# A pair of weight casts moved behind a normalisation on ScalarE, between output projection and up projection

## The chip, the cores and the metric

One Trainium2 chip, one core of it. The time is the device time of one execution in microseconds (us); of several executions the median is given. Engines are called by the names of the profile: PE (TensorE), DVE (VectorE), ACT (ScalarE), POOL (GpSimd) and SP (SyncE, which issues the DMAs here).

## The reference

One decoder layer on 512 tokens of width 1024, in float32, then a last norm. What matters here is the passage from the mixing block to the feed-forward block:

```python
merged = gates[:, :, 0] * y_a + gates[:, :, 1] * y_b + gates[:, :, 2] * y_c
x = x + merged @ w_o                                   # 512x1024 @ 1024x1024
x = x + conv_ffn(rmsnorm(x, ln2_g), w_up, conv_w, conv_b, w_down)
return rmsnorm(x, final_g)

def conv_ffn(u, w_up, conv_w, conv_b, w_down):
    h = causal_dwconv(u @ w_up, conv_w, conv_b)        # 512x1024 @ 1024x5632
    a, v = h[..., :2816], h[..., 2816:]
    return (silu(a) * v) @ w_down
```

`rmsnorm(x, g)` is `x * rsqrt(mean(x*x) + 1e-6) * g` along the 1024 columns. The norm with `ln2_g` is the "second norm": nothing of `u @ w_up` can be computed for a token before its whole row of x is there.

## The kernel before

**Products.** Every large product is computed as three: weights and activations are each split into a high part (a cast to the type that TensorE multiplies) and a low part (what the cast left out), and `mm3` adds high times high, high times low and low times high in PSUM. A product of a weight tile thus needs four things in turn: the raw tile by DMA (`fetch`), its high part `wh` (`cast`, on ACT, as two halves), its low part `wl` (`low`, on DVE, raw minus high), and the activations in both parts.

**Jobs and weight tiles.** `program()` lists some hundred jobs. Each has one weight tile of at most 1 MB and a body that issues the products with it. They share ring buffers: 2 raw tiles (`wraw`), 3 high parts (`whp`), 2 low parts (`wlp`). The loop at the end goes through the jobs; for job n, `prepare` makes the low part of tile n+1, the high part of tile n+2, and fetches tile n+3. A fetch has to wait for a raw buffer, which comes free when the low part of tile n+1 has been made. In most jobs the two casts are not issued at once but one at a time, at the next `step()` of the body (`spread`).

**The order of the work.** PE, ACT, DVE and POOL run their instructions in the order in which the program text issues them (`manual_schedule`), so a waiting instruction holds up everything behind it on its engine. SP's DMAs are put in order by the framework, outside that list.

**Around the change.** The output projection (`wo_jobs`) works on token tiles of 128 rows, in pairs: tiles 0 and 1, then 2 and 3, and for each pair on two halves of 512 columns. Each half is two jobs, one for each half of the inner dimension. When a tile's second half is done, `evac` adds it to x (L939) and begins the norm: squares on ACT (`junk`, L306), the product with g on DVE (`xg`, L339), the mean (`v`, L340), the square root on ACT (L341), then on DVE the reciprocal (L343), two small steps, and the scaled rows (`u`, L347). `norm_turn` then transposes the rows on PE (`uT`, L319), casts them to `uh` on ACT (L322) and subtracts to `ul` on DVE (L323). For tiles 2 and 3 the parts of the norm are kept in the list `late` and are issued by the first two jobs of the up projection.

Three jobs are marked `late`: the last of the output projection (`turn_over`), and the first two of the up projection (`opening`, half 0 and half 1). They call `prepare` themselves. With `later=True` it gives back a function, `rest`, that issues the remaining part when it is called. In the last job of the output projection the call stands ahead of all products, and `rest` is called in `evac` of token tile 3, behind the square root of its norm. In the first job of the up projection the call has `now=False` and everything is in `rest`, which is called behind the transposes of token tile 2.

The first two jobs of the up projection compute only the first 256 tokens (L1036): high weight times `uh`, high weight times `ul`, then the transposes of token tile 2 (in the first job) or 3 (in the second), then low weight times `uh`. The other 256 tokens follow for both jobs together (`held`), through `chunk_a` (L221). `step()` and `up_evac` follow each of these.

Of the kernel before, what the change touches and what calls it, by code (L numbers as in the profile page):

```python
# [81 lines left out]
def trunk(ctx: ExitStack, tc, out, x, rel_bias, ln1_g, w_in, b_gate, w_a, pool_w, pool_scale, w_b,  # L82
# [26 lines left out]
    def MM(name):  # L109
        return psum.tile([P, S], F32, name=name, tag="mm")  # L110
# [26 lines left out]
    def flush():  # L137
        todo = second[:]
        second.clear()
        for f in todo:  # L140
            f()

    def step():
        flush()
        for it in list(running):
            try:
                next(it)
            except StopIteration:
                running.remove(it)
        if waiting:  # L150
            it = iter(waiting.pop(0))
            running.append(it)
            try:
                next(it)
            except StopIteration:
                running.remove(it)
# [11 lines left out]
    def fetch(job, cuts=1):  # L168
        raw = job.raw = wraw.tile([P, job.k, job.c], F32, name="raw", tag="raw")
        at = 0  # L170
        for src in job.parts:
            n = src.shape[-1] // cuts
            for i in range(cuts):
                sp.dma_start(raw[:, :, at:at + n], src[:, :, i * n:(i + 1) * n])
                at += n

    def cast(job, cuts=1, spread=False):

        w = job.c // cuts
        job.high = whp.tile([P, job.k, job.c], F32R, name="wh", tag="wh")  # L180

        def high(i):
            o = slice(i * w, (i + 1) * w)
            act.copy(job.high[:, :, o], job.raw[:, :, o])  # L184

        def at(i):
            high(i)
            if i + 1 < cuts:
                second.append(lambda: at(i + 1))

        if spread:
            second.append(lambda: at(0))
            return
        for i in range(cuts):
            high(i)
# [12 lines left out]
    def low(job, cuts=1, eng=None):  # L208
        for _ in lows(job, cuts, eng):
            pass  # L210

    def wsrc(w, k0, k1, c0, c1):
        return w[k0 * P:k1 * P, c0:c1].rearrange("(k p) c -> p k c", p=P)
# [10 lines left out]
    def chunk_a(ps, ws, j, xh, xl, ks, lo=0, hi=S, k0=0):  # L224
        wh, wl = ws
        mm3(ps[:, lo:hi], lambda k: wh[:, k0 + k, j * P:(j + 1) * P],
            lambda k: wl[:, k0 + k, j * P:(j + 1) * P],
            lambda k: xh(k)[:, lo:hi], lambda k: xl(k)[:, lo:hi], ks)
# [769 lines left out]
    def up_evac(m, ps):  # L998
        t = HC[m] = T("hc")
        act.activation(t, ps, AF.Identity, bias=ff["c1"][:, ff["b"] + m:ff["b"] + m + 1], scale=fw(2, m))  # L1000
        for k in range(2):
            sh = 2 - k
            dve.scalar_tensor_tensor(t[:, sh:], ps[:, :S - sh], fw(k, m), t[:, sh:], OP.mult, OP.add)  # L1003
        if m < KF:
            act.activation(t, t, AF.Silu)
            return
        a = HC[m - KF]
        pool.tensor_tensor(a, a, t, OP.mult)  # L1008

        def later():  # L1010
            yield
            k = m - KF
            if k == 0:
                wide.extend(ypool.tile([P, 4, S], F32R, name=n, tag="xs") for n in ("fh", "fl"))
            h, l = (t[:, k, :] for t in wide) if k < 4 else (T("fh", F32R), T("fl", F32R))
            act.copy(h, a)
            dve.tensor_sub(l, a, h.bitcast(F32))
            ACTS[k] = (h, l)

        running.append(later())  # L1020

    def up_jobs():
        held = []

        def opening(job, half):
            def body(ws):
                uh2, ul2 = nxt["uh"], nxt["ul"]
                low = job.prepare(later=True, now=False) if half == 0 else None
                if half == 0:
                    next(late[1])  # L1030
                pss = [MM("pu") for _ in range(2)]

                def product(a, b, i):
                    for j in range(2):
                        for k in range(KD):
                            pe.matmul(pss[j][:, :256], a[:, k, j * P:(j + 1) * P], b[:, k, :256],  # L1036
                                      start=i + k == 0, stop=i == 2 and k == KD - 1)

                product(ws[0], uh2, 0)
                product(ws[0], ul2, 1)  # L1040
                next(late.pop(0), None)
                if low:
                    low()
                product(ws[1], uh2, 2)
                for j in range(2):
                    held.append((ws, j, pss[j], KF * half + j))
                if half == 0:
                    return
                for n, (ws_, j, ps, m) in enumerate(held):
                    chunk_a(ps, ws_, j, lambda k: uh2[:, k, :], lambda k: ul2[:, k, :], range(KD), 256, S)  # L1050
                    if n == 1:
                        job.prepare()
                    up_evac(m, ps)
                    step()
            return body

        for p in range(KF // 2):
            for half in range(2):
                def body(ws, p=p, half=half):
                    uh2, ul2 = nxt["uh"], nxt["ul"]  # L1060
                    for j in range(2):
                        ps = MM("pu")
                        chunk_a(ps, ws, j, lambda k: uh2[:, k, :], lambda k: ul2[:, k, :], range(KD))
                        up_evac(KF * half + 2 * p + j, ps)
                        step()
                c = half * DFF + p * 256
                job = Job([wsrc(w_up, 0, KD, c, c + 256)], KD, 256, body)
                if p == 0:
                    job.late = True
                    job.body = opening(job, half)  # L1070
                yield job
# [65 lines left out]
    weights = [j for j in jobs if isinstance(j, Job)]  # L1137
# [135 lines left out]
    n = 0  # L1273
    for job in jobs:
        if not isinstance(job, Job):
            job.fn()
            continue
        while second:
            flush()
        if n >= 2:  # L1280
            def prepare(n=n, later=False, now=True):

                def high():
                    if n + 2 < len(weights):
                        cast(weights[n + 2], 2, spread=not later)

                def rest():
                    if n + 1 < len(weights):
                        low(weights[n + 1])
                    if not now or not later:  # L1290
                        high()
                    if n + 3 < len(weights):
                        fetch(weights[n + 3])
                if later:
                    if now:
                        high()
                    return rest
                rest()

            if job.late:  # L1300
                job.prepare = prepare
            else:
                prepare()
            job.body(job.split)
        n += 1
# [38 lines left out]
```

## Time and profile before

| what | value |
|---|---|
| median of 3 runs | 1062.61 us (1062.47 to 1064.94) |
| the profiled execution | 1064.09 us, of which the span of the profile is 1062.2 us |
| PE busy | 1045.9 us, 98% |
| DVE busy | 576.8 us, 54% |
| ACT busy | 431.1 us, 41% |
| POOL busy | 135.1 us, 13% |
| mean granted clock of PE | 0.995 of full speed |
| read from HBM | 110.87 MB, 106 GB/s over the span |

Times in the profile are microseconds from the start of the span; mean durations of single instructions are in nanoseconds. A row of the timeline merges neighbouring instructions of one kind and gives their start, the time that they cover and their number. Matmuls are pipelined, and their ends are modelled: a row's length is a little more than the distance to the next row. The part of the span that the change touches lies between 674 and 710 us.

### The profile page before, as it was taken

The page shows a single profiled execution, that of the slowest core. Times are in us where ns is not written, and L with a number is a line of the kernel's source. Part 1 is how long each engine was busy: PE and PEld are TensorE (multiplying, and loading weights), DVE is VectorE, ACT ScalarE, POOL GpSimd, SP SyncE. Part 2 cuts the span into 40 slices and gives each one's busy share as a digit, 9 for nine tenths or more (in the row PEclk, how much of TensorE's full clock was granted, in tenths as well). Part 3 has the DMA queues.
Part 4 walks back from the last instruction along what each step waited for, and adds up shares of the span by engine and source line. Part 5 has one row for each costly group of instructions (what it writes and reads, how often), then busy time and mean ns, then how long its engine had stood idle before and what let it go on. Part 6 is the DMA issues. An engine that isn't in the chain of part 4 may idle for free.

```text
span 1062.2 us, 13018 instructions
## 1 busy us (share of the span) xinstructions
PE 1045.9 (98%) x5268; PEld 874.4 (82%) x5268; DVE 576.8 (54%) x777; ACT 431.1 (41%) x698; POOL 135.1 (13%) x118
## 2 busy tenths in 40 slices
PE   8999999999999999999999999989999999999997
PEld 8878889888788887787888888888888888888885
DVE  5552523245667547667658766556656565532315
ACT  6343412232445633558536224534444444431311
POOL 1580000000000001100161500002111111110100
PEclk9999999999999999999999999989999999999999
DMA  7236233251221365442243337333232323232312
GB/s 237 79 115 179 82 100 107 72 140 50 83 80 60 83 166 158 110 129 81 80 111 119 119 97 263 119 118 101 95 104 81 118 80 119 80 119 69 110 60 79
DMA packets 116426, 115.50 MB, mean 109 GB/s; under 512 B 5235, under 2 KB 101302, under 8 KB 116367
## 3 DMA queue, kind: packets, MB, share of 16 engines
q1 hardware_dynamic: 116367, 114.68, 35.5%
q8 instruction: 41, 0.67, 0.3%
q14 instruction: 18, 0.15, 0.0%
HBM read 110.87 MB, written 2.22 MB: 106 GB/s over the span
## 4 chain that ended last, share of the span: by engine, by line
PE 91%; ACT 2%; issue 2%; DVE 2%; DMA 1%; POOL 0%; SPq 0%; DVEq 0%; ACTq 0%; POOLq 0%
PE pa L221 35%; PE pu L221 22%; PE pb L221 17%; PE pqk L221 9%; PE ps L512 1%; PE ppw L221 1%; PE po L551 1%; PE pt L539 1%; PE pu L1036 1%; ACT wh L184 1%; PE py L808 1%; DVE wl L204 1%; PE pyo L814 1%; DMA raw<-in_w_in_dram 1%; DMA raw<-in_ffn_w_up_dram 0%
## 5 line engine op out<-in xcount | busy, mean ns | idle before, releaser
L204 DVE TENSOR_TENSOR wl<-raw,wh 128x2048 fp32r<-128x2048 f32 (+3 forms) x94 | 219.2, 2333 | 137.9 <-PE pb L221 67.7
L184 ACT CAST wh<-raw 128x1024 fp32r<-128x1024 f32 (+2 forms) x186 | 187.2, 1025 | 109.6 <-PE pb L221 40.8
L221 PE MATMUL pa<-uh,wh 128*128 128x512 f32 x384 | 99.3, 400 | 0.3 <-ACT wh L184 0.3
L1003 DVE SCALAR_TENSOR_TENSOR hc<-pu,fcol,hc 128x510 f32<-128x510 f32 x88 | 65.9, 749 | 55.9 <-ACT hc L1000 54.3
L221 PE MATMUL pa<-ul,wh 128*128 128x512 f32 x384 | 95.0, 389 | 0.0
L221 PE MATMUL pa<-uh,wl 128*128 128x512 f32 x384 | 94.9, 389 | 0.0
L221 PEld LDWEIGHTS pa<-ul,wh 128*128 128x128 f32 x384 | 72.1, 188 | 15.3
L221 PEld LDWEIGHTS pa<-uh,wl 128*128 128x128 f32 x384 | 72.1, 188 | 15.0
L221 PE MATMUL pu<-ul,wh 128*128 128x512 f32 (+1 forms) x352 | 83.5, 379 | 0.0
L221 PE MATMUL pu<-uh,wl 128*128 128x512 f32 (+1 forms) x352 | 83.5, 379 | 0.0
L221 PE MATMUL pu<-uh,wh 128*128 128x512 f32 (+1 forms) x352 | 83.5, 379 | 0.0
L221 PEld LDWEIGHTS pa<-uh,wh 128*128 128x128 f32 x384 | 69.9, 188 | 16.5 <-issue 1.7
L221 PEld LDWEIGHTS pu<-uh,wl 128*128 128x128 f32 x352 | 64.2, 188 | 12.5
L221 PEld LDWEIGHTS pu<-ul,wh 128*128 128x128 f32 x352 | 64.2, 188 | 12.5
L221 PEld LDWEIGHTS pu<-uh,wh 128*128 128x128 f32 x352 | 64.1, 188 | 12.4
L1000 ACT ACTIVATE hc<-pu,fcol,fcol 128x512 f32<-128x512 f32 x40 | 31.2, 780 | 83.5 <-PE pu L221 83.5
L1008 POOL TENSOR_TENSOR hc<-hc 128x512 f32<-128x512 f32 x22 | 31.6, 1435 | 230.1 <-DVE hc L1003 188.1
L787 POOL TENSOR_TENSOR xd<-xc,dec 128x512 f32<-128x512 f32 x6 | 6.4, 1065 | 361.6 <-DVE xc L778 343.0
L533 ACT ACTIVATE sb<-sb,nm 128x128 f32<-128x128 f32 (+1 forms) x72 | 30.1, 419 | 46.9 <-DVE nm L530 33.2
L221 PE MATMUL pb<-wh,fh 128*128 128x512 f32 x176 | 47.7, 389 | 0.0
L221 PE MATMUL pb<-wl,fh 128*128 128x512 f32 x176 | 47.7, 389 | 0.0
L221 PE MATMUL pb<-wh,fl 128*128 128x512 f32 x176 | 47.7, 389 | 0.0
(273 smaller groups left out, 1601.8 us busy)
## 6 DMA issues: line engine op xcount, KB each, us to landing
raw<-in_w_in_dram SPq DMA_DIRECT2D x25, 1024.0 KB
raw<-in_ffn_w_up_dram SPq DMA_DIRECT2D x22, 1024.0 KB
raw<-in_w_in_dram SPq DMA_DIRECT2D x20, 512.0 KB
raw<-in_ffn_w_down_dram SPq DMA_DIRECT2D x10, 1024.0 KB
raw<-in_w_o_dram SPq DMA_DIRECT2D x8, 1024.0 KB
raw<-in_w_in_dram SPq DMA_DIRECT2D x6, 768.0 KB
raw<-in_w_b_dram SPq DMA_DIRECT2D x4, 1024.0 KB
al<-ad SPq DMA_DIRECT2D x16, 256.0 KB
```

The lines of the kernel that those rows point to most:

```text
L184: act.copy(job.high[:, :, o], job.raw[:, :, o])
L204: (eng or dve).tensor_tensor(l[:, :, o], job.raw[:, :, o], h[:, :, o].bitcast(F32), OP.subtract)
L221: pe.matmul(ps, l, r, start=first and n == 0, stop=last and n == total - 1)
L512: pe.matmul(pss[i][:, o:o + w * P], q[r, n * P:(n + 1) * P], k[r, kb * P:(kb + w) * P], start=True, stop=True)
L533: act.activation(sb[:, off:off + w * P], sb[:, off:off + w * P], AF.Exp, bias=nm[:, n, h:h + 1], accum_out=ls[:, n, h:h + 1])
L539: pe.transpose(pt[:, o:o + P], sb[:, o:o + P], eye)
L551: pe.matmul(po[DH * hh:DH * hh + DH, n * P:(n + 1) * P], V[g, kb + i][:, (2 * c + hh) * DH:(2 * c + hh + 1) * DH], probs[2 * c + hh, nb][: ...
L808: pe.matmul(py[DH * i:DH * i + DH, j * P:(j + 1) * P], xc[:, o:o + DH], als[j // 2][:, lo:lo + P], start=True, stop=True)
L814: pe.matmul(po[:, j * P:(j + 1) * P], prev[gi][:, j * P:(j + 1) * P], XS[10 + gi][:, cs], start=True, stop=True)
L1000: act.activation(t, ps, AF.Identity, bias=ff["c1"][:, ff["b"] + m:ff["b"] + m + 1], scale=fw(2, m))
L1003: dve.scalar_tensor_tensor(t[:, sh:], ps[:, :S - sh], fw(k, m), t[:, sh:], OP.mult, OP.add)
L1008: pool.tensor_tensor(a, a, t, OP.mult)
```

## The change

`prepare` loses its parameter `now` and the function `high`. With `later=True` it issues nothing by itself any more; `rest` issues all: the low part of tile n+1, the two casts of tile n+2, the fetch of tile n+3. The first job of the up projection did that already (by `now=False`), and ordinary jobs issue the three in this order too. So what is different is the last job of the output projection: its two casts, which make the high part of the second weight tile of the up projection, are issued in `evac` of token tile 3, behind the low part of the up projection's first tile, and no longer ahead of the job's products.

```diff
@@ opening, first job of the up projection
-                low = job.prepare(later=True, now=False) if half == 0 else None
+                low = job.prepare(later=True) if half == 0 else None
@@ loop over the jobs
-            def prepare(n=n, later=False, now=True):
-
-                def high():
-                    if n + 2 < len(weights):
-                        cast(weights[n + 2], 2, spread=not later)
+            def prepare(n=n, later=False):
 
                 def rest():
                     if n + 1 < len(weights):
                         low(weights[n + 1])
-                    if not now or not later:
-                        high()
+                    if n + 2 < len(weights):
+                        cast(weights[n + 2], 2, spread=not later)
                     if n + 3 < len(weights):
                         fetch(weights[n + 3])
                 if later:
-                    if now:
-                        high()
                     return rest
                 rest()
```

The calls of it that matter, unchanged:

```python
# jobs_b, last job of the output projection
late_split.append(job.prepare(later=True))
inner(ws)
# wo_jobs, evac of token tile 3
late.append(rest())
late_split.pop(0)()
```

## The prediction

> Names used below: W is the last weight tile of the output projection (token tiles 2 and 3, second half of the columns); U0, U1, U2 are the first three weight tiles of the up projection (U0 and U2 feed the first half of its columns, U1 the second). A tile has a raw form (what the DMA lands), a high part `wh` (two ScalarE casts) and a low part `wl` (one VectorE subtraction). T2 and T3 are the token tiles 2 and 3.
>
> **What bounds the kernel now.** I read the page first, then the waits of TensorE, then the chain of waits around the one place where TensorE stands still, then the engines' timelines there. The page's section 4 gives TensorE nearly the whole chain:
>
> ```profile
> PE 91%; ACT 2%; issue 2%; DVE 2%; DMA 1%; POOL 0%; SPq 0%; DVEq 0%; ACTq 0%; POOLq 0%
> ```
>
> So only what TensorE waits for counts. Its waits (engine, line, waited for: total us, times, longest):
>
> ```profile
> PE pu L1036 <- DVE wl L204: 3.0, 1, 3.0
> PE uT L1217 <- DVE diag L1221: 1.8, 2, 1.5
> PE uT L319 <- DVE u L347: 1.7, 1, 1.7
> ```
>
> The first and third lie together, at the change: the transposes of T2's normalised rows (L319), and the product with U0's low part (L1036). The middle one is at the start and untouched. After 706 us the list of waits has no TensorE row, so whatever is won before 706 moves the rest of the kernel as a block. The chain there (start us, us, what) says who was late:
>
> ```profile
> 681.24 5.20 DMA raw<-in_ffn_w_up_dram
> ...
> 686.54 2.00 ACT wh L184 x2
> 688.54 0.63 ACT junk L306 x2
> ...
> 690.33 1.00 DVE u L347 x2
> 691.34 0.60 DVE x L939
> 691.96 0.73 ACT junk L306 x2
> 692.72 0.16 DVE v L340
> 692.88 2.21 DVE wl L204
> ```
>
> A 1 MB transfer (U1's raw) ends, the two casts of U1 run, and only then the squares of T2's norm (`junk`), its scaling (`u`), T3's residual add and squares, and last U0's low part, which TensorE wants. T2's squares need nothing from the transfer. They stand behind it in ScalarE's queue. VectorE's and TensorE's timelines (start us, us, group, idle before it):
>
> ```profile
> 682.80 0.69 DVE L939 TENSOR_TENSOR x<-x,pb 128x512 f32<-128x512 f32 x1 [1.26 <-PE pb L221]
> 689.19 0.16 DVE L340 SCALAR_TENSOR_TENSOR v<-ss,v 128x1 f32<-128x1 f32 x1 [4.98 <-ACT junk L306]
> ```
>
> ```profile
> 685.32 2.08 PE L1036 MATMUL pu<-uh,wh 128*128 128x256 f32 x16
> 691.02 1.08 PE L319 MATMUL uT<-eye,u 128*128 128x128 f32 x8 [1.72 <-DVE u L347]
> 695.13 3.79 PE L1036 MATMUL pu<-uh,wl 128*128 128x256 f32 x16 [3.03 <-DVE wl L204]
> 698.72 2.67 PE L1036 MATMUL pu<-uh,wh 128*128 128x256 f32 x16
> 701.22 2.09 PE L1036 MATMUL pu<-ul,wh 128*128 128x256 f32 x16
> 703.15 1.03 PE L319 MATMUL uT<-eye,u 128*128 128x128 f32 x8
> 703.94 2.15 PE L1036 MATMUL pu<-uh,wl 128*128 128x256 f32 x16
> ```
>
> T2's row is complete at 683.5, its `v` comes at 689.19: 4.98 us of waiting. The same 16 matmuls take 2.08 at 685.32 and 3.79 at 695.13. The granted clock of that stretch tells why (last columns: clock, DMA share, GB/s):
>
> ```profile
> 693.10:696.60 3.50, 1.47 (x7) 1.47 (x8) 3.32 (x6) 0.98 (x3) 0.00 (x0) 0.51 0.59 166
> 696.60:700.00 3.40, 3.40 (x18) 3.40 (x18) 3.40 (x4) 0.00 (x0) 0.00 (x0) 0.50 0.90 296
> 700.00:703.40 3.40, 3.40 (x30) 3.40 (x30) 0.10 (x1) 2.00 (x2) 0.00 (x0) 1.00 0.58 186
> ```
>
> After the two pauses the clock is half until 700.0.
>
> **The change, part by part.** No instruction is added or removed. In the order of instructions by engine, only ScalarE differs: U1's two casts go from ahead of T2's squares to behind T3's square root, four steps later, ahead of T2's `uh` copies. VectorE, TensorE, GpSimd and SyncE issue what they did, in the same order.
>
> *ScalarE and VectorE without the casts in front.* I carry T2's chain forward with its own offsets. T2's add starts at 682.80. For T3, add to squares is 691.25 to 691.96, or 0.71, so T2's squares start at 683.51. Squares to `v` is 0.76 (691.96 to 692.72): 684.27. `v` to square root 0.19, to reciprocal 0.24, to `u` 0.71 (689.19, 689.38, 689.62, 690.33): `u` at 685.41, complete at 686.41. T3's add follows 0.92 after the start of `u` (690.33 to 691.25): 686.33; TensorE's last matmul for T3 ends at 685.48, so it is not what is waited for. T3's squares 687.04, `v` 687.80, U0's low part at 687.88 (0.08 behind `v`, as 692.72 to 692.80), complete at about 690.17. T3's square root is at 687.99.
>
> *The moved casts.* They follow the square root by 0.11, as the `uh` copies do now: 688.10. Raw U1 has been there since 686.44. The two take 1.91 from start to next start (686.54 to 688.45) and end at 690.1. They cost nothing as long as TensorE wants U1 later, and it does, at 692.1 (below): 2 us of cover. They lie beside U0's low part; today's pair at 679.21 also lies beside a low part (678.93), at 2.00 and 2.29, so no extra cost is charged.
>
> *TensorE.* The two first products with U0's high part run from 685.32, 1.91 each (685.32 to 687.23), to 689.14. Transposes: `u` is long there, 0.79 (703.15 to 703.94), to 689.93. U0's low part lets TensorE start 2.33 after its own start (692.80 to 695.13): 690.21. So a wait of 0.3 stays. Then 1.91 for the low product, to 692.12; two products of U1, to 695.94; T3's transposes 0.79, to 696.73; U1's low product 1.99 (703.94 to 705.93), to 698.7. The next stage, which today starts at 705.93, starts 7.2 us earlier. In parts: pauses of 1.72 and 3.03 less the 0.3 that stays, 4.45; half clock, 3.59 for 1.91 and 2.50 for 1.91 between starts, 2.27; the rest, 0.5, is the drain that a pipelined matmul row shows before each pause.
>
> The clock term is the one that varies. The Trainium skill's page "TensorE: Matmul & The Clock Gate", section "Part 1: The HAM clock gate (the "warmup" mystery)", says that the clock falls to half after an idle window of about 3.4 us, that the window runs freely, and that the loss therefore differs from run to run. The trace agrees on half clock and on steps 3.4 us apart (693.1, 696.6, 700.0), but here two shorter pauses with 1.08 us of transposes between them were enough. By the page's single busy window the loss would be 3.4 us at half rate, 1.7 instead of 2.27, and the sum 6.6, an estimate from that page.
>
> *What moves behind.* SyncE issues final_g's row transfer after T3's `xg` and U2's transfer after U0's low part; both move 4.92 earlier, in today's distance (692.73 and 695.14). U2 landed 5.10 after its issue (its cast starts at 700.24). So its casts are due at 695.32 and take 1.91, to 697.23. Behind them in ScalarE's queue stand T3's `uh` copies, 1.05, to 698.28, and VectorE's `ul` starts 0.62 behind the first copy and takes 1.29, to 699.14. TensorE wants `uh` at 698.7 and `ul` 0.96 later, 699.7 (705.93 to 706.89). The cover is 0.45 and 0.55 us: thin, and what is late next. Today the cast has 1.5 us of rest before those copies.
>
> *Sum.* The profiled execution took 1064.09 (span 1062.2): minus 7.2 gives 1056.9. It is 1.5 over the median, 1062.61. If those 1.5 us are more half clock in this very place than the median run had, its time after is 1056.9 too; if they lie elsewhere, the median gives 1055.4. Nothing in one trace decides it: I take the middle, 1056.2.
>
> **Rivals.** *U2 comes late (8%).* TensorE waits as long as the transfer exceeds 5.10 + 0.45. For it: the cover is thin. Against: two transfers of this stage took 5.20 (681.24 on) and 5.10, and one at most 5.15 (674.06 to 679.21). At 1 to 3 us over, the time is 1057.2 to 1060.
>
> *The second pause stays (5%).* U0's low part stands behind T3's `v` on VectorE. If T3's add or squares were late by some 3 us, only the first pause would go: about 2 us, 1060.6. Against: TensorE is done with T3 0.85 before the add is due.
>
> *Slower (5%).* One mechanism: U2's casts, waiting for their transfer, close ScalarE's queue to T3's copies, as U1's do to T2's squares today. The pause p comes at 698.7, with up to 2.3 us of half clock behind it. It decides from p = 4.9, a landing 10.4 us behind its issue; from there the gain of 7.2 is gone, and at p = 9 the time is 1066 to 1068. Against it are the three times of 5.1 to 5.2; for it, that final_g's row shares the DMA engines, which it does today too.
>
> **How the numbers follow.** The forecast itself has 82%, and its own range is 1054.4 to 1057.2: the low end is 1055.4 less 1 us, if the median run lost more to the clock than the profiled one (two full windows, 3.4 instead of 2.27); the high end is 1056.9 plus the 0.3 of another wait on U0. The range goes up to 1058.9 with two us of the first rival. What the measurement of this kernel can tell from no change is about 0.3%, 3.2 us: faster means below 1059.4. Faster: 82% and 6 of the first rival's 8, 88%. Same: its other 2 and the second rival, 7%. Slower: 5%.
>
> **What would show it.** Right: T2's squares start about 0.7 behind T2's add instead of 5.6; the waits lose the row of `u` L347 and the one of `wl` L204 falls from 3.0 to some 0.3; granted clock 1.00 throughout 693 to 700; U1's casts run without waiting for a DMA; the row of 256-column matmuls of L221 that starts at 705.93 starts near 698.7. Wrong: a new TensorE wait on `uh` or `ul` (U2 late), one on `wh` (U1's casts late), or half clock in spite of the closed pauses.

## The result, and the profile after

| | before | changed |
|---|---|---|
| median | 1062.97 us (4 runs) | 1056.80 us (4 runs, 1055.85 to 1058.24) |
| profiled execution | 1064.09 us, span 1062.2 | 1058.24 us, span 1056.4 |
| ratio | | 0.994, 95% interval 0.9926 to 0.9955 |

The kernel is faster by 6.2 us. In a second series, with 5 and 17 runs, it was 1056.81 against 1063.19 us, ratio 0.9941 (0.9928 to 0.9954). Two executions of the experiments below were far longer, at a lower granted clock (one of `twice`, 1149.67 us at 0.945, and one of the kernel before beside it, 1754.93 us at 0.556), and no ratio counts them.

TensorE's share of the chain is the same 91% as before; there is only less to wait for. What TensorE waited for in the profile after (waited for: total us, times, longest):

```profile
PE pa L1200 <- ACT uh L1187: 1.5, 1, 1.5
PE pa L1148 <- DVE relb L385: 1.1, 1, 1.1
PE pcb L782 <- DVE ea L816: 1.0, 1, 1.0
PE pbt L753 <- ACT o L557: 0.4, 1, 0.4
PE uT L1217 <- DVE diag L1221: 0.4, 1, 0.4
PE pa L221 <- ACT wh L184: 0.3, 1, 0.3
```

The rows of `u` L347 (1.7) and `wl` L204 (3.0) are gone. What is left lies before the stage: at the start of the kernel and in the mixing block. ScalarE's and VectorE's timelines show the cause (start us, us, group, idle before it):

```profile
684.54 0.64 ACT L306 ACTIVATE junk<-x 128x512 f32<-128x512 f32 x1 [2.27 <-DVE x L939]
688.07 0.63 ACT L306 ACTIVATE junk<-x 128x512 f32<-128x512 f32 x1 [2.38 <-DVE x L939]
689.02 0.20 ACT L341 ACTIVATE sq<-v 128x1 f32<-128x1 f32 x1 [0.23 <-DVE v L340]
689.13 1.99 ACT L184 CAST wh<-raw 128x1024 fp32r<-128x1024 f32 x2
697.43 2.00 ACT L184 CAST wh<-raw 128x1024 fp32r<-128x1024 f32 x2 [5.34 <-DMA raw<-in_ffn_w_up_dram]
699.33 1.06 ACT L322 CAST uh<-uT 128x512 fp32r<-128x512 f32 x2
```

```profile
683.82 0.69 DVE L939 TENSOR_TENSOR x<-x,pb 128x512 f32<-128x512 f32 x1 [1.26 <-PE pb L221]
685.29 0.16 DVE L340 SCALAR_TENSOR_TENSOR v<-ss,v 128x1 f32<-128x1 f32 x1
688.90 2.29 DVE L204 TENSOR_TENSOR wl<-raw,wh 128x2048 fp32r<-128x2048 f32 x1
```

T2's squares start 0.72 us behind T2's add (684.54 after 683.82). Before it was 5.65. The casts of U1 (689.13) no longer wait for a DMA. U0's low part starts 5.1 us behind T2's add instead of 10.0. On TensorE:

```profile
686.34 2.08 PE L1036 MATMUL pu<-uh,wh 128*128 128x256 f32 x16
690.17 1.04 PE L319 MATMUL uT<-eye,u 128*128 128x128 f32 x8
691.25 2.17 PE L1036 MATMUL pu<-uh,wl 128*128 128x256 f32 x16
693.26 2.08 PE L1036 MATMUL pu<-uh,wh 128*128 128x256 f32 x16
697.89 2.15 PE L1036 MATMUL pu<-uh,wl 128*128 128x256 f32 x16
699.96 1.23 PE L221 MATMUL pu<-uh,wh 128*128 128x256 f32 x8
```

No row carries an idle time any more, and each run of 16 matmuls takes 2.1 to 2.2 us. The granted clock (last columns: clock, DMA share, GB/s) is whole:

```profile
693.10:696.60 3.50, 3.50 (x31) 3.50 (x30) 3.11 (x3) 0.00 (x0) 0.00 (x0) 1.00 0.77 264
696.60:700.00 3.40, 3.40 (x31) 3.28 (x29) 0.06 (x1) 2.57 (x4) 0.00 (x0) 1.00 0.76 248
```

I call "the stage" what lies between the first product with U0 and the first product of the held tokens. It took 20.61 us (685.32 to 705.93) and now takes 13.62 (686.34 to 699.96): 6.99 us won. The span fell by 5.8 only, because this execution came to the stage 1.02 later (in the mixing block, for one, it has a wait of 1.0 that the profile before has not), and 0.17 went behind it: 1.02 - 6.99 + 0.17 = -5.80.

### The profile page after: what moved, and what is told of

It is laid out like the page before. It is cut to its first block, busy times and chain, and to the rows that moved or that the text cites. A ratio compares the mean times of both kernels' runs of the same rounds, so it can differ in the third digit from the quotient of the medians.

```text
span 1056.4 us, 13018 instructions
## 1 busy us (share of the span) xinstructions
PE 1044.1 (99%) x5268; PEld 872.5 (83%) x5268; DVE 576.7 (55%) x777; ACT 430.9 (41%) x698; POOL 134.9 (13%) x118
## 4 chain that ended last, share of the span: by engine, by line
PE 91%; DMA 2%; issue 2%; ACT 1%; DVE 1%; SPq 1%; POOL 0%; DVEq 0%; ACTq 0%; POOLq 0%
PE pa L221 35%; PE pu L221 22%; PE pb L221 19%; PE pqk L221 7%; DMA al<-ad 1%; PE ps L512 1%; PE pu L1036 1%; PE ppw L221 1%; PE po L551 1%; PE pt L539 1%; DVE wl L204 1%; DMA raw<-in_w_in_dram 1%; SPq L468 1%; PE py L808 1%; PE pyo L814 1%
## 5 line engine op out<-in xcount | busy, mean ns | idle before, releaser
L204 DVE TENSOR_TENSOR wl<-raw,wh 128x2048 fp32r<-128x2048 f32 (+3 forms) x94 | 219.2, 2333 | 137.9 <-PE pb L221 67.6
L221 PE MATMUL pa<-uh,wh 128*128 128x512 f32 x384 | 99.3, 400 | 0.3 <-ACT wh L184 0.3
L221 PE MATMUL pa<-ul,wh 128*128 128x512 f32 x384 | 95.0, 389 | 0.0
L221 PE MATMUL pa<-uh,wl 128*128 128x512 f32 x384 | 94.9, 389 | 0.0
L221 PEld LDWEIGHTS pa<-ul,wh 128*128 128x128 f32 x384 | 72.1, 188 | 15.3
L221 PEld LDWEIGHTS pa<-uh,wl 128*128 128x128 f32 x384 | 72.1, 188 | 14.9
L221 PE MATMUL pu<-uh,wh 128*128 128x512 f32 (+1 forms) x352 | 83.7, 380 | 0.0
L221 PEld LDWEIGHTS pa<-uh,wh 128*128 128x128 f32 x384 | 69.9, 188 | 16.5 <-issue 1.7
L221 PE MATMUL pu<-ul,wh 128*128 128x512 f32 (+1 forms) x352 | 83.5, 379 | 0.0
L221 PE MATMUL pu<-uh,wl 128*128 128x512 f32 (+1 forms) x352 | 83.5, 379 | 0.0
L221 PEld LDWEIGHTS pu<-ul,wh 128*128 128x128 f32 x352 | 64.2, 188 | 12.5
L221 PEld LDWEIGHTS pu<-uh,wl 128*128 128x128 f32 x352 | 64.2, 188 | 12.4
L221 PEld LDWEIGHTS pu<-uh,wh 128*128 128x128 f32 x352 | 64.1, 188 | 12.5
L221 PE MATMUL pb<-wh,fl 128*128 128x512 f32 x176 | 47.7, 389 | 0.0
L221 PE MATMUL pb<-wl,fh 128*128 128x512 f32 x176 | 47.7, 389 | 0.0
L221 PE MATMUL pb<-wh,fh 128*128 128x512 f32 x176 | 47.7, 389 | 0.0
```

What stands on the lines that cost most here:

```text
L204: (eng or dve).tensor_tensor(l[:, :, o], job.raw[:, :, o], h[:, :, o].bitcast(F32), OP.subtract)
L221: pe.matmul(ps, l, r, start=first and n == 0, stop=last and n == total - 1)
```

## Experiments

The theory is that of the prediction: U1's casts waited for their transfer and held T2's squares behind them in ScalarE's queue; two pauses of TensorE followed, and a half clock behind these. The rivals are named in each expectation. All stage lengths below are from the profiles, from the same two matmul rows. In the diffs, calls with a name like `cast_of_U1()` stand for the corresponding part of `prepare`. Where an edit adds lines, line numbers in the rows are 1 to 10 higher (L1039 for L1036, L224 and L325 for L221 and L322).

**The changed kernel again.**

> The changed kernel once more, beside the others of this series, as their measure. 1055.9 to 1058.2 us, 0.994 of the kernel before. The stage from the first product of U0 to the first product of the held tokens takes 13.6 us (20.6 before), TensorE waits 0.3 us or less in it, and its clock stays at 1.00.

Measured: 1056.81 us, 0.9941. Stage 13.56 us (684.86 to 698.42), no TensorE wait from the stage in the list. Of the spread among executions little comes from here: this execution's span is 1.7 us below that of the first profile, with a stage only 0.06 shorter.

**The wait taken away, the casts left in their place.**

```diff
-    wraw = ctx.enter_context(tc.tile_pool(name="wraw", bufs=2))
+    wraw = ctx.enter_context(tc.tile_pool(name="wraw", bufs=3))
-NBIG = 54
+NBIG = 50
```

> The kernel before, with the casts in their old place, but with three raw weight buffers in place of two (and 50 work tiles in place of 54, to make room), so that every fetch is issued a job earlier and U1 lands before its casts come up. Theory of the queue (it was the wait inside the casts, not their place, that held T2's squares back): ScalarE has no wait for U1's transfer, T2's squares start 0.7 us behind T2's add, the stage takes 13.3 to 13.6 us and the time is about 1056, 0.993 to 0.995 of before. Rival (the place of the casts, or their length of 2 us, is what costs): stage and time stay near those of before, 1061 to 1063.

The stage went as the theory of the queue has it: 13.56 us (697.89 to 711.45). ScalarE's timeline shows six casts of half a tile each, in a row and without a wait, done before T2's squares:

```profile
689.49 5.78 ACT L184 CAST wh<-raw 128x1024 fp32r<-128x1024 f32 x6
696.10 0.63 ACT L306 ACTIVATE junk<-x 128x512 f32<-128x512 f32 x1 [0.82 <-DVE x L939]
```

U1's casts are there, and ahead of T2's norm as in the kernel before, and cost nothing. So it was the wait inside them that cost, not their place. But the whole time was missed: 1068.21 us, 1.0042 of before (1.0028 to 1.0056). TensorE's waits between 400 and 640 us, in the mixing block, say where it went:

```profile
PE pxs L776 <- DVE ea L816: 4.1, 2, 2.3
PE pcb L782 <- DVE ea L816: 1.9, 1, 1.9
PE ps L512 <- DVE ea L816: 1.5, 1, 1.5
```

These 7.5 us are not in the profile of before. Three of the four waits are followed by half clock as well (below), so that the mean clock of these 240 us is 0.98, against 1.00 before. The kernel reached the stage 12.6 us later (697.89 against 685.32). The edit changes the order and time of all fetches and the number of work tiles; which of the two delays `ea` was not tried.

**The casts between T2's square root and T3's squares.**

```diff
                 late.append(r2)
+                cast_of_U1()
             else:
                 late.append(rest())
-                low_of_U0(); cast_of_U1(); fetch_of_U2()
+                low_of_U0(); fetch_of_U2()
```

> The changed kernel, with U1's casts one place earlier: behind T2's square root, ahead of T3's squares. Theory of the queue: T2 is free, so the first pause is gone; the casts start when U1 lands, 1.1 us after the end of TensorE's last output product, and end about 1.2 us after T3's squares would have begun; U0's low part and TensorE come 1.2 us later than in the changed kernel, a wait of 1.5 us in place of 0.3, too short for the clock: stage 14.8 us, time 1058.0, 0.995 of before. Rival (any place behind T2's squares is as good, or the gain came from elsewhere): 13.6 us and 1056.8.

Measured: 1057.95 us, 0.9951 (0.994 to 0.9963), against 1058.0 expected. Stage 14.86 us (685.28 to 700.14), with the pause where it was expected:

```profile
691.51 2.17 PE L1039 MATMUL pu<-uh,wl 128*128 128x256 f32 x16 [1.36 <-DVE wl L204]
```

So T2's half of the move brings 5.7 us of the 7.0 and T3's half the rest, through U0's low part: what a place costs depends on what still stands behind the transfer there. At a pause of 1.36 the clock stayed at 1.00.

**The clock by itself: both pauses filled with idle matmuls, in the kernel before.**

```diff
+                if half == 0:
+                    idle = SM("idle")
+                    def keep(n):
+                        for _ in range(n):
+                            pe.matmul(idle[:, :256], ws[0][:, 0, :P], uh2[:, 0, :256], start=True, stop=True)
+                    keep(12)
                 next(late.pop(0), None)
                 if low:
                     low()
+                    keep(22)
```

> The kernel before, with 12 and 22 matmuls of no use (high weight of U0 times uh, 256 columns, into a PSUM tile that nobody reads) put on TensorE into the two pauses, ahead of T2's transposes and ahead of U0's low product. At 0.12 us each they take 1.4 and 2.6 us, less than the pauses of 1.72 and 3.03. Theory of the prediction (two pauses plus a half clock that they bring about): the pauses stay, the clock stays at 1.00 to 700 us, the stage falls from 20.6 to 18.3 us, and the time by 2.3 us, to 0.998 of before (1060.7 if before is 1063.0). If the half clock does not come from the pauses: the stage stays at 20.6 us or grows, and the time is that of before.

Measured: 1061.80 us, 0.9986 (0.9977 to 0.9994). Stage 18.41 us (685.36 to 703.77), 2.20 less than before, clock 1.00:

```profile
691.01 1.06 PE L319 MATMUL uT<-eye,u 128*128 128x128 f32 x8 [0.22 <-DVE u L347]
691.83 2.87 PE L1046 MATMUL idle<-uh,wh 128*128 128x256 f32 x22
695.12 2.18 PE L1036 MATMUL pu<-uh,wl 128*128 128x256 f32 x16 [0.43 <-DVE wl L204]
```

T2's transposes and U0's low product start where they did (691.0 and 695.1); what changes is the two rows behind: 16 matmuls in 2.18 and no longer 3.79, the next 16 in 2.08 and no longer 2.67. The half clock was its own part of the sum, 2.2 us in the profiles. Over all runs the saving is 0.14%, about 1.5 us; its interval, 0.06 to 0.23% or 0.6 to 2.4 us, takes in the 2.2.

**Which pause lowers the clock.** The same edit with one `keep` only.

> The kernel before, with the 12 idle matmuls in the first pause only; the second, of 3.0 us, stays open. If the second pause alone brings the clock down: half clock behind it, stage 20.0 to 20.6 us. If it takes both pauses with little between them: clock 1.00, stage 18.4 us as with both filled.

> The kernel before, with the 22 idle matmuls in the second pause only; the first, of 1.7 us, stays open. A pause of 1.4 us did not lower the clock in the kernel with the casts between the two norms, so clock 1.00 and a stage of 18.4 us. If a pause of 1.7 us is enough: half clock behind it, in the idle matmuls or later.

With the first pause filled, the second (3.05 us) is enough:

```profile
694.14 3.78 PE L1036 MATMUL pu<-uh,wl 128*128 128x256 f32 x16 [3.05 <-DVE wl L204]
697.72 2.97 PE L1036 MATMUL pu<-uh,wh 128*128 128x256 f32 x16
```

Stage 20.77 us (684.46 to 705.23), 1063.40 us. With the second filled, the first (1.56 us) does nothing to the clock: stage 18.30 us (684.70 to 703.00), 1061.21 us. So in these two executions the second pause was enough and the first was not.

That pauses of such lengths always act so doesn't follow, and the profile with three raw buffers speaks against it. There the waits of 2.33, 1.93 and 1.51 us in the mixing block each brought half clock, and one of 1.77 did not. What tells them apart is where they lay. In slices of a tenth of a microsecond the clock fell at 441.18, 461.66 and 499.21 us, up to 1.8 us after the wait had ended, and rose at 444.60, 465.08 and 502.62. Counted from the first, these times are 0, 6, 17, 1, 7 and 18 times 3.413 us. So the clock changes only at the borders of steps of 3.41 us. The three waits lay whole inside the step before the fall; the wait of 1.77 was divided by a border (478.73) into 0.60 and 1.17. In the profiles of the kernel before, the fall and the rise lie two such steps apart, and the step before the fall (689.79 to 693.20) holds 1.23 us of the first pause and 1.10 of the second.

**The kernel before, profiled again.**

> The kernel before, profiled once more. The two pauses are there again (1.7 and 3.0 us). If the half clock behind them follows a window that runs freely, it begins and ends at another place of the stage than 693 to 700 us, and the stage's length differs from 20.6 us by up to 1 us; if it hangs on the pauses alone, both are the same as in the first profile.

Measured: 1063.33 us, stage 20.34 us (684.81 to 705.15), pauses 1.67 and 3.03. In slices of half a microsecond the clock is 0.50 from 692.2 to 699.0; in the first profile it was from 693.2 to 700.0. Both times 6.8 us, which begin 0.6 and 1.1 us into the second pause. So the stretch does sit differently, and the stage differs by 0.27 us. Here the step that ends at the fall (688.75 to 692.16) holds the whole first pause, 1.67 us, and only 0.60 of the second: the fall can't be put down to the second pause alone in this execution.

**U2 made late, with its casts ahead of T3's copies.**

```diff
-                    sp.dma_start(raw[:, :, at:at + n], src[:, :, i * n:(i + 1) * n])
+                    for _ in range(2 if twice else 1):      # twice for U2 only
+                        sp.dma_start(raw[:, :, at:at + n], src[:, :, i * n:(i + 1) * n])
```

> The changed kernel, with U2's raw tile fetched twice into the same buffer, which makes U2 land some 5 us later; nothing else is changed. This is the prediction's case of a slower kernel, made on purpose: U2's casts stand ahead of T3's uh copies on ScalarE. Theory of the queue: landing 10.3 to 11.5 us after the first issue, T3's copies begin about 4 us later than in the changed kernel, TensorE pauses 3.5 to 5 us ahead of the held tokens, and its clock may go to half for up to 2.3 us more: 1060.5 to 1064, at or near the kernel before (ratio 0.998 to 1.001). Rival (the transfer is hidden, since U2 itself is wanted only 11 us later): 1056.8.

> U2 fetched twice, its casts ahead of T3's copies, for an undisturbed profile of it: its median was 1063.38, 6.6 us over the changed kernel. A pause of TensorE on T3's uh of 3.5 to 4.5 us, then half clock for some 3.4 us or more (1.7 to 2.3 us lost); together the 6.6 us. If the clock stays at 1.00, the pause alone must be 6 us or more.

Measured: 1063.38 us, 0.9998 (0.9989 to 1.0007): the whole gain is gone. The profile is that of the second expectation, an execution of 1063.43 us:

```profile
700.40 1.99 ACT L187 CAST wh<-raw 128x1024 fp32r<-128x1024 f32 x2 [9.46 <-DMA raw<-in_ffn_w_up_dram]
702.30 1.07 ACT L325 CAST uh<-uT 128x512 fp32r<-128x512 f32 x2
```

```profile
702.93 2.08 PE L224 MATMUL pu<-uh,wh 128*128 128x256 f32 x8 [4.03 <-ACT uh L325]
704.80 1.91 PE L224 MATMUL pu<-ul,wh 128*128 128x256 f32 x8
706.51 1.88 PE L224 MATMUL pu<-uh,wl 128*128 128x256 f32 x8
708.22 1.13 PE L224 MATMUL pu<-uh,wh 128*128 128x256 f32 x8
```

The pause of 4.03 makes the stage 17.75 us, 4.19 longer than in the changed kernel's second profile. The first 24 matmuls behind it take 1.87, 1.71 and 1.71 us from start to start instead of 0.96 each, another 2.41. Together 6.6; the difference of the medians is 6.4 (1063.23, without the long execution, less 1056.81).

**U2 as late, its casts behind T3's copies.** The double fetch stays; U2's casts move behind the second call of T3's norm generator:

```diff
                 next(late.pop(0), None)
                 if half == 0:
                     low_of_U1(); fetch_of_U3()
+                else:
+                    cast_of_U2()
```

> U2 fetched twice as in the run before last, and its casts behind T3's uh copies. Theory of the queue: the late transfer now holds up only U2's own casts, wanted 11 us later, and the first evacuations of the held tokens by under 2 us, which have four PSUM banks of room: no pause, clock 1.00, 1056.8 as without the second transfer. Rival (the late transfer itself costs, by U2's casts or by the DMA queue): 1060.5 to 1064, as with the casts ahead.

Measured: 1056.06 us, 0.9931 (0.9918 to 0.9945), stage 13.56 us (684.40 to 697.96), no pause.

```profile
695.81 1.08 ACT L325 CAST uh<-uT 128x512 fp32r<-128x512 f32 x2 [5.66 <-PE uT L322]
699.61 2.00 ACT L187 CAST wh<-raw 128x1024 fp32r<-128x1024 f32 x2 [2.72 <-DMA raw<-in_ffn_w_up_dram]
```

U2's casts begin 10.29 us after its first issue (689.32), against 10.30 (690.10 to 700.40) in the run before. The same late transfer, at a place where only its own casts wait for it, costs nothing.

**The same order, U2 fetched once.**

> The changed kernel, with U2's casts put behind T3's uh copies on ScalarE. T3's copies then wait for the transposes alone. In the trace of the changed kernel U2 landed 6.15 us after its issue, more than the 5.55 for which the prediction had room, and the first 8 held matmuls took 1.06 us in place of 0.96. Theory: that 0.1 us goes, 1056.7, not to be told from 1056.8 by time; T3's copies begin about 1.7 us earlier. If the copies were not late at all: no difference.

Measured: 1056.31 us, 0.9934 (0.9921 to 0.9946), stage 13.56 us (684.45 to 698.01). T3's copies begin at 695.86, 0.64 behind the transposes' start, where they began 2.23 behind it in the changed kernel's first profile. The first 8 held matmuls take 0.96 instead of 1.06; but they do so in the changed kernel's second profile too, where U2 landed earlier. By time this order can't be told from the changed kernel.

**U0's low part, U1's casts and U2's fetch ahead of T3's add.** U2's casts stay behind T3's copies here.

```diff
             t = X1[tb, h]
+            if pair == 1 and h == 1 and tb == 3:
+                low_of_U0(); cast_of_U1(); fetch_of_U2()
             dve.tensor_tensor(t, t, ps, OP.add)
```

> U2's casts behind T3's uh copies, and also U0's low part, U1's casts and U2's fetch ahead of T3's residual add. U0's low part then starts when T2's rows are scaled, about 1.5 us earlier, and is ready before TensorE has finished T2's transposes; U1's casts end before T3's squares are due. Theory: the last wait in the stage (0.3 us) goes, stage 13.2 to 13.3 us, 1056.4; by time it can't be told from the changed kernel. Rival: T3's norm, now 2.2 us later, is late for its transposes or U1's low part (done 1 us ahead of use by the offsets of the trace) and TensorE waits there: 1057 or more.

Measured: 1056.68 us, 0.9935 (0.9923 to 0.9948). Stage 13.24 us (685.53 to 698.77), as expected; the low product follows the start of the transposes by 0.79 us (689.36 to 690.15) where it was 1.08. This is the shortest stage measured, and the 0.3 us are lost in the spread of the runs. By time the changed kernel and the three versions with U2's casts behind T3's copies can't be told apart (medians 1056.06 to 1056.81; the intervals of their ratios overlap).

## Why the prediction was right

**The order alone moves, and only on ScalarE.** Right. T2's squares were forecast 0.71 behind T2's add and came at 0.72; U0's low part was forecast 5.08 behind it (687.88 after 682.80) and came at 5.08 (688.90 after 683.82).

**The casts cost nothing in the new place.** Right. They end at 691.1, 2.1 us ahead of the first product with U1 (693.26); the forecast was 2.

**TensorE: 7.2 us.** Measured 6.99 and 7.05. The remaining wait at U0's low product was forecast as 0.3; the transposes start 1.08 before it, 0.29 more than their 0.79. The terms that were too short are the two low products: U0's took 2.01 us to the next row (691.25 to 693.26) instead of 1.91, and U1's 2.07 (697.89 to 699.96) instead of 1.99.

**The clock: 2.27 of these.** Right in size (2.20 with the pauses filled). The prediction read "steps 3.4 us apart (693.1, 696.6, 700.0)" out of its table; these are the borders of the windows that it asked for, and the clock did not change at 696.6. It fell at 693.20, inside the second pause, and rose at 700.03. That there are such steps is shown only by the later profiles. Of the two pauses the prediction made no choice; in both profiles of before the step ahead of the fall holds parts of both, and the second was enough by itself where the first was filled. The estimate from the Trainium skill's page, 1.7 us and a sum of 6.6, was too low for the profiled executions: the half clock lasted 6.8 us both times, not 3.4, because the second pause reached into the step behind the fall, and the matmuls began 1.9 and 2.4 us into it.

**What moves behind: U2's cover of 0.45 to 0.55.** The mechanism was right, one of its sizes was off. U2 landed 6.18 us after its issue (691.25 to 697.43), beyond the 5.55 that the prediction allowed, yet the first held product came only 0.07 later for it (2.07 for U1's low product, 2.00 in the second profile), and its 8 matmuls took 0.10 more. The prediction wanted both of T3's copies done; by the kernel's text the first 4 matmuls of a product need only the first. So the true cover is some 0.5 us more: a landing at 6.18 with 0.07 lost and one at 10.30 (U2 fetched twice) with 4.19 lost both put its end at 6.11. The duration was mis-sized, too. From one row, 5.10, I took the transfer as fixed. From issue to cast it was 5.10, 5.34, 5.45, 5.86 and 6.97 in five profiles of the old order of casts, and 5.19, 5.27 and 6.18 in three with U1's casts behind T2's squares. By this working a transfer of 6.97 would cost the changed kernel nearly 0.9 us, an estimate; neither of its two profiles has one.

**The rivals.** "U2 comes late" was on the edge: its condition, a transfer over 5.55, was met in one of two profiles, but its price was 0.2 us there and not 0.6. "The second pause stays" did not happen. "Slower" was priced rightly: the prediction put the point from which the gain is gone at a pause of 4.9 us with 2.3 of half clock behind it, 7.2 in all. With U2 fetched twice, a pause of 4.03 with 2.4 of half clock gave 6.6 and a ratio of 0.9998.

**The base of the sum.** The prediction took the middle between 1056.9 (profiled execution) and 1055.4 (median) and forecast 1056.2; measured were 1056.80 and 1056.81. The choice was a matter of luck in part: with 7.2 us taken from the median alone the forecast would have been 1.4 us too low. The reason that it offered for the scatter, more half clock in the stage, holds for 0.27 of the 0.76 us between the two profiled executions of before. The changed kernel, without any half clock there, scatters as widely (1055.85 to 1058.24), and its two profiles differ in the waits before the stage. The medians moved by 6.2 and 6.4 us, less than the 7.0 of the stage; the interval of the second series, 4.9 to 7.7 us, takes in all three, and whether the half clock cost the median execution less than the profiled ones was not settled.

## What to carry to other kernels

Look at what an in-order engine has queued behind an instruction that waits for a DMA: the transfer may be needed much later by its own consumer and still stop the kernel through its neighbours. Either put the waiting instruction behind the work on the critical path, or make the transfer land before it; both gave the same stage here, but the edit for the second also moved every other transfer and took four work tiles away, and lost more than it won. Price a pause of TensorE with the clock behind it, and check which instruction the next late transfer would hold up.

## What the runs showed of the hardware

In five profiles the granted clock of TensorE changed, and only at the borders of steps of 3.41 us, counted in each profile from its own first change (what lies behind the last product is left aside): six changes in the mixing block with three raw buffers (0, 1, 6, 7, 17 and 18 steps), and a fall and a rise two steps apart in the stage of four others (693.20 to 700.03, 692.16 to 698.99, 692.92 to 699.74 and 701.40 to 708.23). In the step that ended with a fall TensorE had stood still for 1.51 to 2.50 us in these seven cases. Steps with up to 1.4 us of it kept the clock, and so did the one with the pause of 1.56 us that was left open beside the filled one; between 1.5 and 1.8 us the runs don't say what decides. The half clock lasted one step where the next step was busy throughout (3.4 us, behind waits of 1.51 to 2.33 us) and two where the pause reached into it by 1.2 to 2.4 us (6.8 us, behind pauses of 3.03 to 4.03 us). So of three waits of similar length (1.51, 1.77 and 1.93 us) two brought 3.4 us of half clock and one nothing: a pause can't be priced by its length alone.

The Trainium skill's page "TensorE: Matmul & The Clock Gate", section "Part 1: The HAM clock gate (the "warmup" mystery)", gives an idle window of about 3.4 us as the condition. The runs agree on the length of the window, but it need not be idle throughout: 1.51 us of 3.41 were enough once. They agree with the prediction's other point from that section, that the window runs freely: in the two profiles of before the second pause begins 6.78 and 6.75 us behind the start of the stage, and the fall comes at 7.88 and 7.35.

The same 1 MB transfer, issued at the same point of the program behind the same smaller one, took from 5.1 to 7.0 us from its issue to its first cast in eight profiles. A cover of half a microsecond is within that spread.
